# Sending the first store of a rotary-embedding kernel as two transfers, of 4 rows and of 12 rows

## Chip, cores, metric

One core of a Trainium2 chip. The metric is the device time of one execution in microseconds (us), lower is better. Differences within 2% count as the same. The program has one core, so its profile has no second die to compare with; all timed runs quoted here were marked fast, except that a single-run profile (run 8) is marked unknown. The span, by contrast, is the time from the program's first instruction to its last; the timed figure is 1.6 to 2.3 us longer.

## The reference

```python
batch, seq, heads, dim = (16, 512, 16, 64)          # x: float32, 33.55 MB
x1, x2 = x[..., :32], x[..., 32:]
cos, sin = cos[None, :, None, :], sin[None, :, None, :]
rotated_first  = x1[..., :16] * cos[..., :16] - x1[..., 16:] * sin[..., :16]
rotated_second = x1[..., :16] * sin[..., :16] + x1[..., 16:] * cos[..., :16]
return np.concatenate([rotated_first, rotated_second, x2], axis=-1)
```

Each element is read once and written once: 67.11 MB of traffic, and four vector operations on half of it.

## The kernel before

The rows of `x` are cut into T = 4 tiles of 8.39 MB. A tile has K = 16 rows of 4 KB on each of 128 partitions, so one partition's part of a tile is a contiguous run of 64 KB in memory. The kernel keeps three tiles on the chip at a time (the ring), and tile 3 takes the slot of tile 0. All loads and stores of `x` go through one queue, that of SP (`nc.sync`), and SP works through its instructions in order: a store that waits for the vector engine holds up what comes after it (the second half of load 2 waits for nothing, and is issued at 43.77 us, right behind store 0 at 43.37).

```python
K = 16; NS = 3; KC = K // 2; K0 = K // 4; R = H * D          # 8, 4, 1024
ring = const_pool.tile([P, NS, K, H, D], fp32)

def load(t, lo=0, hi=K):
    nc.sync.dma_start(out=rows(t, lo, hi), in_=xf[t, :, lo * R : hi * R])

def store(t, lo=0, hi=K):
    nc.sync.dma_start(out=of[t, :, lo * R : hi * R], in_=rows(t, lo, hi))
# ... cut: the two small tables, 64 KB each, on another queue ...
load(0, 0, K0)
load(0, K0, K)
load(1)
load(2, 0, KC)
# ... cut: the tables are spread over the partitions ...
rotate(0, 0, K0)                      # in place, four vector operations each
rotate(0, K0, (K0 + K) // 2)
rotate(0, (K0 + K) // 2, K)
store(0)
load(2, KC, K)
load(3)                               # takes tile 0's slot: waits for store(0)
for t in range(1, T):
    rotate(t, 0, KC)
    rotate(t, KC, K)
    store(t)
```

## Time and profile before

| | before |
|---|---|
| median of 3 runs, us | 162.55 (162.50 to 162.89) |
| span of the profiled run, us | 160.9 |
| DVE busy | 112.9 us, 70% |
| moved | 67.24 MB, 418 GB/s over the span |

The lines that carry the reading stand in the prediction. One more is of use, the list of what the vector engine (DVE) waited for; its columns are engine, line, what it waited for, us in total, times, longest:

```profile
DVE spun L74 <- DMA stage<-in_sin_dram: 8.7, 1, 8.7
DVE b_t L98 <- DMA ring<-in_x_dram: 5.2, 2, 4.9
```

DVE waits for a load of `x` twice in 160.9 us, 5.2 us in all, and at the start 8.7 us for the sine table.

### The profile page before, as it was taken

What the parts mean: (1) busy time and instruction counts of PE and PEld (TensorE: products, weight loads), DVE (VectorE), ACT (ScalarE), POOL (GpSimd) and SP (SyncE); (2) the same over time, 40 slices, a digit from 0 to 9 for tenths busy, and PEclk for the clock granted to TensorE, in tenths of its full rate; (3) what the DMA queues carried; (4) which work ended last, traced back from release to release, by engine and by line L of the source; (5) the groups of instructions that cost most, each with busy time, mean ns of one, the idle gap of its engine ahead of it and who ended that gap; (6) DMA issues with size and microseconds to landing.
All of it is one profiled execution on the core that took longest, in us unless ns stands there. A gap on an engine that the chain in (4) does not pass through costs nothing.

```text
span 160.9 us, 116 instructions
## 1 busy us (share of the span) xinstructions
DVE 112.9 (70%) x47; POOL 1.4 (1%) x6
## 2 busy tenths in 40 slices
DVE  1049999999999999999999991699999900000000
POOL 3000000000000000000000000000000000000000
DMA  6999999969999996999996996998998998998992
GB/s 195 554 391 391 391 456 521 521 261 521 391 391 261 521 521 261 521 391 391 472 570 261 521 521 261 521 423 358 521 423 358 521 423 358 521 423 358 521 423 98
DMA packets 1504, 67.24 MB, mean 418 GB/s; under 512 B 192, under 2 KB 192, under 8 KB 224
## 3 DMA queue, kind: packets, MB, share of 16 engines
q1 hardware_dynamic: 1440, 67.11, 97.7%
q0 software_dynamic: 64, 0.13, 0.2%
HBM read 33.69 MB, written 33.55 MB: 418 GB/s over the span
## 4 chain that ended last, share of the span: by engine, by line
DMA 50%; DVE 28%; DVEq 1%; issue 0%; SPq 0%
DMA ring<-in_x_dram 31%; DMA out_dram<-ring 18%; DVE b_t L98 10%; DVE ring L99 10%; DVE ring L100 5%; DVE ring L103 3%; DVEq L142 1%; SPq L55 0%; DVEq L98 0%
## 5 line engine op out<-in xcount | busy, mean ns | idle before, releaser
L98 DVE TENSOR_TENSOR b_t<-ring,table 128x4096 f32<-128x4096 f32 (+2 forms) x9 | 35.6, 3959 | 5.4 <-DMA ring<-in_x_dram 5.2
L99 DVE TENSOR_TENSOR ring<-ring,table 128x4096 f32<-128x4096 f32 (+2 forms) x9 | 35.6, 3950 | 0.3
L100 DVE TENSOR_TENSOR ring<-ring,b_t 128x2048 f32<-128x2048 f32 (+2 forms) x9 | 18.4, 2049 | 0.3
L103 DVE TENSOR_TENSOR ring<-ring,b_t 128x2048 f32<-128x2048 f32 (+2 forms) x9 | 18.4, 2042 | 0.0
L74 DVE LOAD_MASK_SELECT spun<-stage x1 | 0.0, 14 | 8.7 <-DMA stage<-in_sin_dram 8.7
L84 DVE COPY table<-packed 32x1024 f32<-32x1024 f32 x4 | 2.7, 684 | 0.1
L81 DVE COPY packed<-spun 32x512 f32<-32x512 f32 (+3 forms) x4 | 1.7, 416 | 0.1
L61 DVE MEMSET stage<- 128x512 f32 x1 | 0.5, 485 | 0.9 <-PEq L131 0.9
L74 DVE STREAM_SHUFFLE spun<-stage 128x512 f32<-128x512 f32 x1 | 0.7, 722 | 0.0
L63 POOL DMA_DIRECT2D stage<-in_cos_dram x1 | 0.6, 649 | 1.3 <-DVE stage L61 1.3
L64 POOL DMA_DIRECT2D stage<-in_sin_dram x1 | 0.5, 532 | 0.0
L131 POOL MEMSET const-bfloat16-1.0<- 128x1 bf16 x1 | 0.1, 96 | 0.0
L131 POOL MEMSET const-float32-0.0<- 128x1 f32 x1 | 0.1, 93 | 0.2 <-issue 0.2
L131 POOL MEMSET const-float32-1.0<- 128x1 f32 x1 | 0.1, 93 | 0.0
L131 POOL MEMSET const-uint8-127<- 128x1 uint8 x1 | 0.1, 93 | 0.0
## 6 DMA issues: line engine op xcount, KB each, us to landing
ring<-in_x_dram SPq DMA_DIRECT2D x2, 4096.0 KB, 44.9
ring<-in_x_dram SPq DMA_DIRECT2D x1, 6144.0 KB, 21.6
ring<-in_x_dram SPq DMA_DIRECT2D x1, 2048.0 KB, 7.7
stage<-in_cos_dram POOLq DMA_DIRECT2D x1, 64.0 KB, 6.3
stage<-in_sin_dram POOLq DMA_DIRECT2D x1, 64.0 KB, 7.7
out_dram<-ring SPq DMA_DIRECT2D x4, 37.2
ring<-in_x_dram SPq DMA_DIRECT2D x2, 34.7
```

What stands on the lines that cost most here:

```text
L61: nc.vector.memset(stage[:, :, :, 0:Q], 0.0)
L63: nc.gpsimd.dma_start(out=spread[:, 0, 0], in_=cosf)
L64: nc.gpsimd.dma_start(out=spread[:, 0, 1], in_=sinf)
L74: nc.vector.stream_shuffle(out=spun[:], in_=stage.rearrange("p t k j -> p (t k) j")[:, :, 0:Q], mask=[j % PQ * REP for j in range(PB)],)
L81: nc.vector.tensor_copy(out=packed[0:n], in_=spun[q * PB : q * PB + n])
L84: nc.vector.tensor_copy(out=table[r * PB : (r + 1) * PB].rearrange("p t k c j -> p (t k) c j"), in_=packed.unsqueeze(2).to_broadcast((PB, ...
L98: nc.vector.tensor_mul(out=b_t, in0=x1, in1=s)
L99: nc.vector.tensor_mul(out=x1, in0=x1, in1=c)
L100: nc.vector.tensor_sub(out=x1[:, :, :, 0:Q], in0=x1[:, :, :, 0:Q], in1=b_t[:, :, :, Q:HF])
L103: nc.vector.tensor_add(out=x1[:, :, :, Q:HF], in0=x1[:, :, :, Q:HF], in1=b_t[:, :, :, 0:Q])
L131: nc = _bacc.Bacc("TRN2", target_bir_lowering=False, num_devices=1)
L142: with _tile.TileContext(nc) as tc:
```

## The change

The intent, as the code shows it: rows 0 to 3 of tile 0 are ready long before the rest, so let them leave at once, and let only the other 12 rows wait for the last rotation.

```diff
     rotate(0, 0, K0)
     rotate(0, K0, (K0 + K) // 2)
     rotate(0, (K0 + K) // 2, K)
-    store(0)
+    store(0, 0, K0)
+    store(0, K0, K)
     load(2, KC, K)
     load(3)
```

Below, "small store" and "larger store" are these two. A transfer "lands" when its last bytes have arrived.

## The prediction

> **What bounds the kernel now.** The kernel moves 33.55 MB in and 33.55 MB out through one queue and does a little vector work between. I read the page's second, third and fourth parts first, to see whether the transfers or the vector engine set the time:
>
> ```profile
> DVE  1049999999999999999999991699999900000000
> DMA  6999999969999996999996996998998998998992
> ...
> HBM read 33.69 MB, written 33.55 MB: 418 GB/s over the span
> ...
> DMA 50%; DVE 28%; DVEq 1%; issue 0%; SPq 0%
> ```
>
> The vector engine (DVE) is done at four fifths of the span, the transfers fill it to the end. The chain of waits gives DVE 28% of the span all the same, so I asked whether that share is real: the chain in order of time, and the waits of the queue that issues the transfers (SP).
>
> ```profile
> 1.17 21.62 DMA ring<-in_x_dram
> ...
> 43.37 29.64 DMA out_dram<-ring
> ...
> 73.03 28.86 DMA ring<-in_x_dram
> ```
>
> ```profile
> SPq L58 <- DVE ring L103: 62.2, 3, 26.9
> SPq L58 <- DMA ring<-in_x_dram: 33.1, 3, 20.2
> SPq L142 <- DMA out_dram<-ring: 30.6, 1, 30.6
> SPq L55 <- DMA out_dram<-ring: 28.8, 1, 28.8
> ```
>
> By the chain, the first store is issued at 43.37 us, when the third rotation of tile 0 ends, and takes 29.64 us. The 8.39 MB that it moves take other stores 19.3 us. The other 10 us are a place in the line: the loads issued before it have not finished. So the DVE stretch from 22.8 to 43.4 us is only the chain's way of walking back; a store issued earlier would have waited longer in the queue.
>
> The packet records of the trace settle it. One transfer is 8 packets on each of 16 engines, a packet being one partition's contiguous run. The landings (mean over the engines) and the time since the landing before are: load 0, rows 0-3, 8.14 us; load 0, rows 4-15, 22.62 (14.48 later); load 1, 41.97 (19.35); load 2 first half, 53.05 (11.07); store 0, 72.85 (19.80); load 2 second half, 82.10 (9.25); load 3, 101.59 (19.49); store 1, 120.95 (19.36); store 2, 140.27 (19.32); store 3, 159.58 (19.31). That is strictly the order of issue, and there is no gap between neighbours: a 64 KB packet takes 2.418 us, eight take 19.34 us, which is the whole distance of two landings.
>
> So the span is a sum: 67.11 MB at 433.6 GB/s (65,536 B in 2.418 us on each of 16 engines) is 154.8 us; the first landing comes 3.3 us later than its 2.10 MB need (issue, first packets, the two small table loads); load 2's first half comes 1.4 us later than its 9.67 us; about 0.1 us elsewhere; and 1.3 us from the last mean landing to the end. Together 160.9, the span. The timed median, 162.55, is 1.65 us more.
>
> The 1.4 us are the only irregularity in the middle. The windows around it show it:
>
> ```profile
> 41.00:47.80 6.80, 6.77 (x3) 0.00 (x0) 1.00 1.07 463
> 47.80:52.60 4.80, 4.73 (x3) 0.00 (x0) 1.00 0.85 246
> 52.60:72.00 19.40, 19.26 (x7) 0.00 (x0) 1.00 1.01 439
> ```
>
> The last column is GB/s (bytes are booked at a packet's start, so a short window is rough). The last two rounds of 32 KB load packets before the first store take up to 2.36 us instead of 1.21. Load 3, the other load that a store follows, slows in its last round alone: mean 2.67 us for 2.418, up to 2.84. Where load follows load, or load follows store, nothing of that size is seen.
>
> **What the Trainium skill says.** "DMA: Bandwidth & Descriptors", section "Queues, rings and completion order": on each engine descriptors are consumed in ring order. The trace agrees: the second half of load 2 was issued at 43.77 us with nothing to wait for, and its packets start near 71.8 us, behind store 0. The same page, "Where 436 GB/s comes from", puts the ceiling at 435.2 GB/s; the 433.6 of the full packets is that ceiling within half a per cent, so nothing is to be had from the steady part. The same page, "Anatomy of one DMA — SWDGE (gpsimd) path", gives each DMA a fixed cost of about 2 us, mostly the receipt of the last byte, for DMAs of another issuing path than this one. No such cost shows between queued transfers here (19.31 to 19.36 us between stores whose packets need 19.34), so one DMA more should not cost it. The same page, "Latency and other measured facts", reports copies that fall to half rate or less at HBM row pitches of 512 KiB and more; here rows of 16 KB would be written at a pitch of 64 KB, which is outside the range that it measured. The trace has the reading side of just this shape: the load of rows 0-3 has a median packet of 0.611 us, near full rate.
>
> **The change part by part.** Removed: one store of 128 runs of 64 KB. Added: a store of 128 runs of 16 KB and one of 128 runs of 48 KB, same bytes, same places.
>
> 1. Issue. The small store needs only the first rotation (rows 0-3), which ends at 22.55 us, so it is issued near 22.6 instead of 43.37. SP has nothing else to issue there. The larger store still waits for the third rotation and goes at about 43.4. SP's extra issue costs about 0.35 us (the four stores' issues take 0.332 to 0.379), while SP is idle: zero on the path.
>
> 2. Place in the line. Loads 0, 1 and the first half of 2 were issued by 2.63 us and last until 53. At 22.6 load 1 is just starting. The small store goes behind load 2's first half, exactly where its bytes stood before. Its bytes move no earlier. Gain: zero.
>
> 3. Packets. Per engine, before: 8 x 2.418 = 19.344 us. After: 8 x 0.608 (the fastest 16 KB packets) + 8 x 1.815 (all 48 KB packets) = 19.384 us. Loss 0.04 us, and one completion packet of 9 ns more.
>
> 4. What waits for the store. Load 3 takes the ring slot of tile 0, so it waits for both stores and goes out near 73.1 instead of 73.03 us. At that time load 2's second half still has 9 us in the queue, so the queue does not run dry. DVE next starves at 97.1 us for 4.86 us before tile 3, whose rotations end at 128.84, while the last store's packets begin only at about 140. Another 0.04 us vanishes in those 11 us.
>
> 5. The 1.4 us at the turn from loading to storing. The change touches this place: store packets of 16 KB, issued 30 us ahead of the turn instead of 10, will follow load 2. I cannot derive the sign. If late issue causes the slowdown, it goes (load 3's turn, whose store was issued 27 us ahead, lost only about 0.2 us). If small packets cause it, it stays or grows. I book an average gain of 0.2 us.
>
> Sum: 162.55 + 0.04 - 0.2 = about 162.4 us.
>
> **The rivals.**
>
> - The earlier store relieves the ring, load 3 starts earlier, DVE's 4.86 us wait goes and the time drops by several us. For it: the chain names store 0 and load 3 for 58 us together. Against: load 3 is behind load 2's second half and needs both stores; and the queue has no hole that an earlier load 3 could fill. It would make 158 to 160 us. I give it 1 in 100.
> - The turn is cured: 1.2 to 1.4 us less, 161.2 us. For it: load 3's turn with an early store is mild. Against: that turn has larger load packets too, so the issue time is not singled out. About 3 in 10. It is still within 2%.
> - Short runs written at a 64 KB pitch go slowly, or the turn gets worse with small packets. At half rate the small store would take 9.7 us instead of 4.9, so 167.4 us. Against: the same runs are read at full rate, and the full-size stores write at the ceiling. A loss over 3.25 us is 2 in 100; a loss of 0.3 to 1.5 us about 1 in 10.
> - The in-place rotation of rows 4-15 waits until the small store has read its rows: then DVE would idle from 22.9 to about 58 us and the time would grow by more than 10 us. Against: the kernel before already rotates rows 0-3 (from 15.54 us) while the load of rows 4-15 into the same tile is in flight (it lands at 22.8), so waits are set by rows and not by tile. Under 1 in 100.
>
> **Range and chances.** Two per cent is 3.25 us. The three runs before lie within 0.39 us, and all that I can name except unlikely slow writes moves less than 1.5 us. The low end is the cured turn with noise, 161.1; the high end a turn worse by half, 163.2. Faster by over 2%: 0.02; within 2%: 0.96; slower: 0.02.
>
> **What would show it right or wrong.** Right: store issues near 22.6 and 43.4 us; the order of landings unchanged, the small store about 58 us, the larger near 73; 16 KB store packets at about 0.61 us; load 3 landing at about 101.6 and the span between 159.5 and 161.5. The window 47.8 to 52.6 tells about the turn. Wrong: store packets of 16 KB well over 0.61 us, DVE idle after 22.9 us, any hole in the DMA row near 57 us, or the small store's packets mixed in among the loads' before 50 us.

## The result

| | before | after |
|---|---|---|
| median of 4 runs each, us | 162.72 | 163.00 (162.91 to 163.06) |
| ratio, 95% interval | 1 | 1.0016 (0.9997 to 1.0035) |
| span of the profiled run, us | 160.9 | 160.9 |
| packets of the x queue | 1440 | 1584 |

Ratios are the mean time of one kernel's runs over that of the other's in the same rounds, so not quite the ratio of the medians.

The time is the same. From the page of the changed kernel, the busy rows of the two engines in 40 slices, then two of the issues (KB each, us from issue to landing):

```profile
DVE  1049989999999999999999991699999900000000
DMA  5999999969999999989996996996996996996990
...
out_dram<-ring SPq DMA_DIRECT2D x1, 6144.0 KB, 29.4
...
out_dram<-ring SPq DMA_DIRECT2D x1, 2048.0 KB, 35.6
```

The small store takes 35.6 us from issue to landing. By its eight rounds of packets it needs 4.9; the rest is waiting in line. From the timeline of the queue (start, length of the stretch, what was issued, how many):

```profile
0.74 1.86 SPq L55 DMA_DIRECT2D ring<-in_x_dram  x4
22.43 21.32 SPq L58 DMA_DIRECT2D out_dram<-ring  x2
43.79 29.36 SPq L55 DMA_DIRECT2D ring<-in_x_dram  x2
```

The small store is issued at 22.43 us, 21 us earlier than the whole store was. And the chain of waits, in order of time, at the places shown of before:

```profile
1.17 21.65 DMA ring<-in_x_dram
...
43.40 29.35 DMA out_dram<-ring
...
72.81 29.03 DMA ring<-in_x_dram
```

It is the chain of before: the larger store still leaves at 43.40 and is done at 72.75 (before: the whole store at 73.02), and load 3 follows. The packet records give the same: load 2's first half lands at 52.84 us (mean over the engines), the small store at 57.73, the larger one at 72.56, load 3 at 101.40, store 3 at 159.35 (before 159.58). The order is the order of issue; the 21 us were spent in the queue.

The turn from loading to storing, in windows of the changed kernel (start:end, length, DVE busy, POOL busy, clock, DMA share, GB/s):

```profile
41.00:47.80 6.80, 6.76 (x3) 0.00 (x0) 1.00 1.05 453
47.80:52.60 4.80, 4.73 (x3) 0.00 (x0) 1.00 0.90 276
52.60:72.00 19.40, 19.26 (x7) 0.00 (x0) 1.00 1.03 443
```

Before it was 246 GB/s in the middle window, now 276: the slow place is still there. The records size it: the last two rounds of load packets took 1.24 us more than the usual 2 x 1.213 (before 1.37, and in a second profile of before 1.24).

### The profile page after: what moved, and what is told of

Same layout as the page of the kernel before. It is cut to its first block, busy times and chain, and to the rows that moved or that the text cites. A ratio compares the mean times of both kernels' runs of the same rounds, so it can differ in the third digit from the quotient of the medians.

```text
span 160.9 us, 120 instructions
## 1 busy us (share of the span) xinstructions
DVE 112.9 (70%) x47; POOL 1.4 (1%) x6
## 3 DMA queue, kind: packets, MB, share of 16 engines
q1 hardware_dynamic: 1584, 67.11, 97.6%
## 4 chain that ended last, share of the span: by engine, by line
DMA 50%; DVE 28%; DVEq 1%; issue 0%; SPq 0%
DMA ring<-in_x_dram 31%; DMA out_dram<-ring 18%; DVE b_t L98 10%; DVE ring L99 10%; DVE ring L100 5%; DVE ring L103 3%; DVEq L143 1%; SPq L55 0%; DVEq L98 0%
## 5 line engine op out<-in xcount | busy, mean ns | idle before, releaser
L98 DVE TENSOR_TENSOR b_t<-ring,table 128x4096 f32<-128x4096 f32 (+2 forms) x9 | 35.6, 3959 | 5.5 <-DMA ring<-in_x_dram 5.3
L99 DVE TENSOR_TENSOR ring<-ring,table 128x4096 f32<-128x4096 f32 (+2 forms) x9 | 35.6, 3950 | 0.3
## 6 DMA issues: line engine op xcount, KB each, us to landing
out_dram<-ring SPq DMA_DIRECT2D x1, 2048.0 KB, 35.6
```

What stands on the lines that cost most here:

```text
L98: nc.vector.tensor_mul(out=b_t, in0=x1, in1=s)
L99: nc.vector.tensor_mul(out=x1, in0=x1, in1=c)
```

## The experiments

Twelve runs. "Turn loss" is always the sum, over the rounds of load packets just before a store, of their mean duration less the usual one (1.213 us for 32 KB, 2.418 us for 64 KB), from the packet records. These are read from the trace file itself, as no view lists single packets: sorted by their starts, each 16 packets of a transfer, one for each engine, are a round. The edits of runs 2, 3, 9 and 11 are against the changed kernel, those of runs 4 to 7, 10 and 12 against the kernel before; every ratio is against the kernel before. ACT (`nc.scalar`) is the scalar engine, whose queue this kernel does not otherwise use.

### 1. The change again, more rounds

No edit.

> The changed kernel itself, timed in more rounds, as the median of its first four runs was 0.28 us over that of before and its interval (0.9997 to 1.0035) did not tell that from nothing. My theory (the store's bytes keep their place in the line; packets cost 0.04 us more): ratio 1.0003, the interval holding 1.000, and below 1.002. Rival (an extra transfer, or short runs, cost something that the packet records do not show): ratio 1.0015 to 1.003 with an interval wholly above 1.0005.

162.91 us against 162.70, ratio 1.0018 (1.0002 to 1.0035): nearer to the rival's numbers than to mine. The record lists the span of every timed run: 160.72 us in the mean of these six, 160.62 for before. So of the 0.27 us between the mean times only 0.10 lie inside the span, and 0.17 outside it. See run 12 for what such a difference is worth.

### 2. The small store really ahead in the line

```diff
     load(1)
-    load(2, 0, KC)
 ...
     rotate(0, 0, K0)
+    store(0, 0, K0)
+    load(2, 0, KC)
     rotate(0, K0, (K0 + K) // 2)
     rotate(0, (K0 + K) // 2, K)
-    store(0, 0, K0)
     store(0, K0, K)
```

> The changed kernel with the first half of load 2 issued after the small store instead of before it, so that the small store really goes ahead in the line: its packets must then follow load 1 (landing near 47 us instead of 57.5) and load 2's first half follows it. Theory that the line is full and only the sum of bytes counts: time within 1% of before, whatever the order; load 3 lands within 2 us of 101.6. Rival (an earlier landing of the store is worth something): at least 1.5 us faster. It also has two turns from load to store. If the 1.3 us at the turn belong to the first store of the program, they move to the turn after load 1 and the second turn (32 KB load packets) loses under 0.4 us. If they belong to 32 KB load packets ahead of a store, the turn after load 1 loses about 0.2 and the turn after load 2's half again 1.3. If each turn costs, the time grows by up to 1.3 us.

163.04 us, ratio 1.0025 (1.0008 to 1.0042). The small store landed at 48.2 us, 9.5 us earlier than in the changed kernel, and load 3 at 101.3. Landing earlier is worth nothing. The turn loss moved: 1.20 us in the one round of 64 KB packets before the small store, and 0.01 us where the larger store follows 32 KB load packets. So load packets of 32 KB are not its cause. Windows of this run, around the small store's start:

```profile
34.00:38.80 4.80, 4.77 (x2) 0.00 (x0) 1.00 1.01 437
38.80:43.60 4.80, 4.65 (x4) 0.00 (x0) 1.00 0.99 321
43.60:48.40 4.80, 4.76 (x2) 0.00 (x0) 1.00 1.03 444
48.40:53.20 4.80, 4.77 (x2) 0.00 (x0) 1.00 1.01 437
```

The dip is now at 38.8 to 43.6 us; at 47.8 to 52.6, where both kernels had it, there is none.

### 3. Without most of tile 0's vector work (wrong result)

```diff
     rotate(0, 0, K0)
-    rotate(0, K0, (K0 + K) // 2)
-    rotate(0, (K0 + K) // 2, K)
     store(0, 0, K0)
```

> Wrong result on purpose: the rotations of rows 4 to 15 of tile 0 are left out, so the larger store has only its load to wait for and is issued near 23 us instead of 43.4. Theory (20 us of vector work in the chain of waits are no bound, the line is): time within 0.5% of before, landings of store 0 (about 72.5 us) and load 3 (101.5) where they were. Rival (the chain's DVE share of 28% is real): 15 to 20 us faster. For the turn: if it is slow because the store is issued late, its loss falls from 1.3 us to about 0.2; if not, it stays between 1.0 and 1.5.

162.46 us, ratio 0.9989 (0.9971 to 1.0006); the result was wrong, as meant. The busy rows, and the chain in order of time:

```profile
DVE  1049950000499999999999990699999900000000
DMA  5999999969899999989996996996996996996990
```

```profile
1.17 21.77 DMA ring<-in_x_dram
...
22.95 49.76 DMA out_dram<-ring
...
72.78 28.96 DMA ring<-in_x_dram
```

20 us of vector work are gone from the path that the chain named, and the end has not moved. The larger store, issued at 22.95 instead of 43.4 us, now takes 49.76 us instead of 29.35 and lands at 72.71 us, as before. The DVE stretch of the chain was never a bound. The turn loss is 1.15 us although both stores wait in line 25 us ahead of the turn: a late issue is not its cause either.

### 4. The first store as 16 stores of one row

```diff
-    store(0)
+    for r in range(K):
+        store(0, r, r + 1)
```

> The first store as 16 stores of one row, with runs of 4 KB. Theory that a queued transfer costs only its packets: 4 KB packets took 0.159 us for the small tables, so 128 of them need 20.35 us per engine instead of 19.34; time up by about 1.0 us (ratio 1.006), and under 2 us. Rival (each extra transfer pays a fixed cost of around 2 us in the line): up by 20 us or more. Rival (short runs are written slower than they are read): 4 KB store packets clearly over 0.159 us, time up by several us. If the turn depends on the size of the store's first packets, its loss changes from 1.3 us by more than 0.5.

163.87 us, ratio 1.0075 (1.0054 to 1.0095), some 1.2 us more. From the landing of the load before them to the last of the 16 landings 20.62 us pass, where one store took 19.80; a 4 KB packet took 0.159 us in the median, as predicted, and only the last two of the 16 stores were slower (1.67 and 1.39 us between landings; the others 1.21 to 1.29, for 1.27 us of packets). SP issued seven of the 16 stores by 42.2 us and each later one when an earlier transfer had landed, still some 10 us ahead of its own landing, so the queue did not run dry. A fixed cost for each queued transfer does not show: the spans of the four runs are 1.46 us longer than those of before in the mean, and what the packets leave of that is 0.03 us for each of the 15 extra stores. The turn loss is 1.06 us with 4 KB store packets behind: their size is not its cause.

### 5 to 7. A tiny store at the start

The kernel before, with 8 KB of zeros stored early to a place that store 3 writes over; in run 7 copied inside the chip memory instead.

```diff
+    zero = const_pool.tile([16, 128], fp32)
+    nc.vector.memset(zero[:], 0.0)
 ...
     load(0, 0, K0)
+    nc.sync.dma_start(out=of[3, 0:16, 0:128], in_=zero[:])      # run 5
 ...
+    nc.scalar.dma_start(out=of[3, 0:16, 0:128], in_=zero[:])    # run 6, ahead of the table loads
+    nc.scalar.dma_start(out=spare[:], in_=zero[:])              # run 7, in run 6's place
# ... cut: run 7's tile `spare`, of the shape of `zero` ...
```

> The kernel before, with one extra store of 8 KB (16 runs of 512 B of zeros, one for each transfer engine; the last store writes over them) issued by SP between the two loads of tile 0. In the run with the small store ahead, the 1.2 us lost at the turn went with the first store of the program, and the later turn after 32 KB load packets lost nothing. Theory (the first store of a program costs 1.2 us once): the turn before store 0 now loses under 0.3 us, and 0.5 to 1.2 us are lost near 8 us instead; time the same within 0.5 us. If the early loss falls beside the start of the queue and costs nothing, the time is 1.0 to 1.3 us lower (ratio 0.992 to 0.994). Rival (the first turn with large stores costs, whatever stored before): the turn still loses 1.0 to 1.5 us, time up by 0 to 0.5 us.

> The same tiny store issued by ACT, on a queue of its own, at the very start. Theory: the first-store cost is paid there while the SP queue's loads go on, so the turn before store 0 loses under 0.3 us and the time falls by 0.8 to 1.3 us (ratio 0.992 to 0.995). If an engine stalls for all of its queues, the loss moves to the first load packets, time the same. Rival (large stores' first turn costs anyway): turn 1.0 to 1.5 us, time the same.

> A control: the same 8 KB from ACT at the start, but copied to another SBUF tile instead of stored to memory. If the turn's loss is the first write to the output (HBM), it stays at 1.0 to 1.5 us and the time is that of before. If it is the first read of SBUF by the transfer engines, it falls under 0.3 us as with the tiny store.

Turn losses 1.29, 1.18 and 1.17 us; medians 163.09, 162.98 and 162.90 us; ratios 1.0024, 1.0018 and 1.0014. The tiny packets ran at 7.5 to 7.9 us in run 5, 4.7 to 5.3 us in run 6 and 5.4 to 5.9 us in run 7. My theory, that the first store of a program pays once, however small, fell in both of its runs. I had hoped for a kernel 1 us faster from it; there was none.

### 8. The kernel before, profiled again

No edit.

> The kernel before, profiled once more: how far a profile differs from itself. Turn before store 0 losing 1.2 to 1.5 us, span 160.5 to 161.0. If the loss is gone or doubled here, it is no property of the program and the runs above have to be read again.

Span 160.7 us, turn loss 1.24 us. It belongs to the program, and two profiles of one kernel differ by 0.13 us in it.

### 9. The small store on a queue of its own

```diff
     rotate(0, 0, K0)
+    nc.scalar.dma_start(out=of[0, :, 0 : K0 * R], in_=rows(0, 0, K0))
     rotate(0, K0, (K0 + K) // 2)
     rotate(0, (K0 + K) // 2, K)
-    store(0, 0, K0)
     store(0, K0, K)
```

> The changed kernel with the small store issued by ACT, on a queue of its own, as soon as rows 0 to 3 are rotated (22.6 us). Theory (the engines are full, only the sum of bytes counts): its packets mix with those of load 1, load 1 lands about 4.9 us later (46.8 for 42.0), everything after store 0 lands where it did, time within 0.5% of before. Rival (the small store gains when it need not stand in line): 1.5 us or more faster. For the slowdown ahead of the first large store: the three tiny-store runs showed that a store of 8 KB at 3 to 6 us does not take it away. If it goes with the length of the unbroken run of loads before a store (21 MB: 1.3 us; 12.6 MB: 0.2; 4.2 MB: 0), the turn at 48 us, now 12 us after the small store's last packets, loses under 0.3 us, and the mixed stretch loses 0 to 1.2.

162.65 us, ratio 0.9983 (0.9966 to 0.9999). The records show the packets of the two queues taking turns one by one: the first six small-store packets start 3.0 to 3.1 us apart, which is 2.418 + 0.611. Load 1 lands at 47.1 us instead of 41.9, the small store at 48.9, load 3 at 101.2. What the small store gains load 1 pays. No load slows before the larger store any more, and 0.97 us are lost in three rounds of load 1 during the mixing. The spans of its six runs are 160.48 us in the mean (160.2 to 160.9) against 160.89 (160.7 to 161.4): 0.41 us shorter. The profile is of the longest of the six, so no trace shows where the shorter ones gain.

### 10. The tiny store 5 us before the turn

The kernel before, with the 8 KB stored by ACT after the last rotation of tile 0.

```diff
     rotate(0, (K0 + K) // 2, K)
+    nc.scalar.dma_start(out=of[3, 0:16, 0:128], in_=rows(0, K - 1, K)[0:16, 0:128])
     store(0)
```

> The kernel before with the tiny store (8 KB, ACT) at 43.4 us, 5 us before the turn, instead of at the start. If the slowdown comes from the time since the last write, however small, the turn loses under 0.4 us. If it needs a large store or goes with the length of the run of loads, it still loses 1.0 to 1.5 us. Time within 0.5% of before either way.

163.31 us against 162.94, ratio 1.0021 (1.0003 to 1.0039). The tiny packets ran at 47.4 to 48.9 us, and store 0's first packets start at 52.5. Turn loss 1.33 us: the time since the last write, however small, is not it.

### 11. The small store after 12.6 MB of loads

```diff
-    load(1)
-    load(2, 0, KC)
+    load(1, 0, KC)
 ...
     rotate(0, 0, K0)
+    store(0, 0, K0)
+    load(1, KC, K)
+    load(2, 0, KC)
     rotate(0, K0, (K0 + K) // 2)
     rotate(0, (K0 + K) // 2, K)
-    store(0, 0, K0)
     store(0, K0, K)
```

> The changed kernel with load 1 in two halves and the small store between them, so that the first turn comes after 12.6 MB of loads instead of 21.0 (before) or 16.8 (small store ahead), the same length as ahead of store 1, which loses 0.1 to 0.25 us. If the loss goes with the length of the run of loads, the first turn loses under 0.4 us, and so does the one after the rest of load 1 and load 2's half (8.4 MB): time 0.8 to 1.2 us lower than the changed kernel's. If the first large store costs 1.2 us wherever it stands, the first turn (near 30 us) loses 1.0 to 1.4 and the time is the changed kernel's.

163.31 us, ratio 1.0024 (0.9995 to 1.0053). The turn loss at the small store is 1.50 us, and 0.24 us at the larger one. Windows around the first of them:

```profile
24.00:28.80 4.80, 4.76 (x2) 0.00 (x0) 1.00 1.01 437
28.80:33.60 4.80, 4.73 (x4) 0.00 (x0) 1.00 0.94 270
33.60:38.40 4.80, 4.77 (x2) 0.00 (x0) 1.00 1.11 474
```

The dip comes at 29 us, as soon as a store of 2 MB stands there. The theory of the length of the run of loads fell: after the same 12.6 MB, store 1 of the kernel before loses 0.25 and 0.11 us in its two profiles.

### 12. A control for small differences

```diff
+    idle = const_pool.tile([P, 16], fp32)
     nc.vector.memset(stage[:, :, :, 0:Q], 0.0)
+    for _ in range(4):
+        nc.vector.memset(idle[:], 0.0)
```

> All variants with one transfer more came out 0.2 to 0.4 us slower in the timed runs (ratios 1.0014 to 1.0025) while their profiled spans did not grow; each also has 3 or 4 instructions more in the trace. Control: the kernel before with 4 tiny DVE memsets more, in the time in which DVE waits for the tables, and no transfer more (120 instructions as in the changed kernel). If instructions cost it: ratio 1.0014 to 1.0025. If the extra transfer costs it: ratio 0.9995 to 1.0005.

162.60 us against 162.94, ratio 0.9979 (0.9963 to 0.9994): four instructions that do nothing of use, in time in which DVE waits anyway, came out 0.34 us faster with an interval clear of 1. Neither of my two readings had that. The spans say where it lies: 160.92 us in the mean against 160.89. So the whole difference is outside the span (1.68 us of the time, 2.05 in before). Builds differ there by about 0.2% of the time for reasons that these runs don't show, and the 0.3 us of the change are no larger than that.

## Why the prediction was right

**The bound.** Right, and runs 2, 3 and 9 show it rather than argue it: the store's bytes moved 9.5 us ahead, 20 us of vector work removed, two queues instead of one, and each time load 3 landed at 101.2 to 101.3 us and the time stayed within 0.25% of before.

**Issue (step 1).** Right: 22.43 and 43.40 us for 22.6 and 43.4.

**Place in the line (step 2).** Right: the small store landed at 57.73 us for "about 58", behind load 2's first half.

**Packets (step 3).** Right in kind. Each 16 KB packet took 0.611 us, not the fastest 0.608, so the two stores' packets need 19.41 us for 19.34, a loss of 0.06 instead of 0.04. Of the two stores' 19.72 us between landings (4.89 + 14.83, before 19.80) it cannot be seen.

**What waits for the store (step 4).** Right: load 3 was issued after the landing at 72.75, the queue did not run dry, and DVE's wait for a load was at most 4.8 us, before 4.9. Nor did the rotation of rows 4 to 15 wait for the small store: it began at 22.91 us.

**The turn (step 5).** This term failed. The prediction booked "an average gain of 0.2 us" there; the loss was 1.24 us in the changed kernel (1.13 in run 1, the same kernel) and 1.37 and 1.24 in the two profiles of before: no gain that stands clear of the difference between two profiles of one kernel. Both causes that it named are ruled out: late issue by run 3, small packets by run 2 for the loads and run 4 for the store. Without this term the sum reads 162.6. The forecast "within 2%" did not rest on it: the term is 0.1% of the time, and even the full cure would have stayed within 2%. So being right there says nothing for step 5.

**What remains.** The measured median is 0.6 us over the predicted one: 0.2 from the turn's gain that did not come, about 0.2 because before itself came out at 162.72 instead of 162.55 in the same rounds, and some 0.2 that the packets don't explain. In run 1, the same kernel, 0.17 us of the difference lie outside the span, where no packet of `x` moves. Run 12, with 0.37 us less there after four idle instructions, says not to read a cause into this part.

**Still open: the turn loss itself.** Shown: where the small store led, its start carried the loss, after 12.6 MB of loads (1.50 us) and after 16.8 MB (1.20), with load packets of 32 and of 64 KB; the larger store, when it came second, lost 0.24 us or less, and store 1 lost 0.30 us or less in every profile. The size of the store's packets, the time of its issue, and tiny writes at 5, 8 and 48 us do not change it. Nor is it DVE's work beside the transfers: DVE was busy for 4.77 of 4.80 us between 48.4 and 53.2 us of run 2 and went on so to 58, and the second turn in that time lost 0.01 us. Why the first large store of the program costs this, and no kernel here got rid of it, stays open. No version beat both kernels clearly. Run 9 is ahead of before by 0.17% in time, no more than the control; but its 0.41 us lie inside the span and the control's outside, so a gain of some 0.4 us there may be real. Whether it comes from its smaller loss is not shown.

## What to carry to other kernels

When a transfer takes much longer from issue to landing than its bytes need, ask first what stands before it in the queue: issuing it earlier then only lengthens its wait. The chain of waits follows the last releaser of each step, so it can lead through an engine whose removal changes nothing; check the bytes against the steady rate before believing its shares. And before giving a cause to a difference of some tenths of a per cent, run a control that changes nothing that matters, and see whether the difference lies inside the span at all.

## What the Trainium skill lacked or had wrong

- No page has a loss when a program turns from loads to its first large store. Here it was 1.06 to 1.50 us in all thirteen profiles in which that store stood in line behind loads (run 9, with two queues, is left out), and 8 KB written earlier did not prepay it.
- "DMA: Bandwidth & Descriptors", section "Anatomy of one DMA — SWDGE (gpsimd) path": its fixed cost of about 2 us for each DMA is given for the other issuing path, and that section does not say what is left of it behind other queued work. Here 16 queued stores of 0.52 MB took 20.62 us in all, with 20.35 us of packets.
- The same page, "Queues, rings and completion order": an engine is said to drain a packet of typically some 9 to 17 descriptors from one queue before it turns to the next. In run 9 two queues, while both had work, took turns after every single run, of 64 KB and of 16 KB (starts 3.0 to 3.1 us apart). The trace does not show how many descriptors a run has, so it says only that a turn was one run long.
